# One weight tile and three general tiles more, paid for with a smaller reserve for software DMA descriptors, and other prices in a list scheduler

## The chip, the cores and the metric

One core of one Trainium2 chip runs the whole kernel in one launch. The metric is device microseconds of that core. The engines are called as in the profile: PE (TensorE, matmuls), PEld (its weight loads), DVE (VectorE), ACT (ScalarE), POOL (GpSimd, which here only issues DMAs) and SP (SyncE, which only issues DMAs). A measurement of this kernel tells a difference of about 0.3% from none.

## The reference, cut to what matters

The input is 512 tokens of width 1024, with 16 learned meta tokens ahead of them, so T = 528. Two layers run after one another.

```python
for l in range(DEPTH):                                # DEPTH = 2
    n = rms_norm(h, mix_norm_g[l])
    proj = jnp.einsum("btd,de->bte", n, w_in[l])      # q, k, v, indexer qi/ki/wi, xr, yg, cv, gates gt
    attn = dsa_attention(q, k, v, qi, ki, wi)         # indexer scores, top-128 keys, softmax
    rnn  = rg_lru_branch(xr, yg, ...)                 # conv 4, block-diagonal gates, scan
    cnv  = conformer_conv_branch(cv, ...)             # GLU, depthwise conv 31, LayerNorm, swish
    merged = (g_attn * jnp.einsum("bte,ed->btd", attn, w_o_attn[l])
              + g_rnn * jnp.einsum("bte,ed->btd", rnn, w_o_rnn[l])
              + g_conv * jnp.einsum("bte,ed->btd", cnv, w_o_conv[l]))
    h = h + jnp.einsum("btd,de->bte", merged, w_out[l])
    f = rms_norm(h, ffn_norm_g[l])
    a = jax.nn.silu(f @ w_ffn_gate[l]) * (f @ w_ffn_up[l])
    h = h + a @ w_ffn_down[l]
return h[:, N_META:]
```

All of it is float32, and nearly all of the arithmetic is in products of activations with weights.

## The kernel before, in words

**Layout.** Activations lie transposed: 128 channels on the partitions, 528 tokens (512 in the second layer, after its projections of keys and values) along the free axis. A weight block of 128 output channels by 1024 input channels is one DRAM transfer of 512 KB into a tile of 128 x 1024.

**Products in three passes.** A float32 operand is split into a high part, rounded to float32r, and a low part, the rest. `gemm` (L554 on) multiplies, for each of the 8 slices of 128 input channels, the weight's high part with both parts of the activation (L568: two matmuls, or with 528 columns two of 264 columns for each, so 32 of 264 columns in a weight block), and then, in a second pass over the 8 slices, the weight's low part with the activation's high part (L578: 16 of 264 columns). The products of the conformer's output and of most of the feed-forward layer go through `seven` (L609 high, L613 low), a seven-product scheme on half-size blocks, whose factors are formed from four quarter blocks.

**How a weight comes in.** `weights_in` lets SP load the block into one of two `raw` tiles (L397). `weights_split` takes a `w` tile, and ACT copies the block into it, rounded (the high part, L376). Then it takes a second `w` tile for the low part. For some blocks DVE subtracts (L379). For the others (`by_dma`) ACT writes the negative of the raw block into the tile, and POOL issues a software DMA (L400) that reads the same block from DRAM once more and adds it on the way. There are four `w` tiles, so two weights. `gemm` gives the high part's tile back after the first pass and the low part's after the second:

```python
            hi = yield Alloc("w", 1, FR)
            yield act(hi[:, :k], r[:, :k], AF.Copy, [r], [hi])
            hbox.set(hi)
            lo = yield Alloc("w", 1, FR)
            ...
                yield act(lo[:, :k], r[:, :k], AF.Copy, [r], [lo], scale=-1.0)
                free(r)
                yield add_dma(lo[:, :k], src, [], [lo])
```

In `seven` the low parts of three of the seven factors come by the same kind of DMA, into general `s` tiles (128 x 528, 77 of them), which hold nearly everything else too.

**What sets the order.** Nothing is ordered by hand. Every piece of work is a generator that yields either an operation with a price in ns or a request for tiles. `Sched.run` plays these streams against a clock for each engine: it takes the operation that could start first, or, within 40 ns and on the same engine, the one of the best priority, issues its instruction, and moves that engine's clock by the price. Prices of PE, DVE and ACT come from the tile's width. For a transfer it keeps one clock of bytes moved, at 360 bytes per ns, and holds the result to be there 1900 ns (`MOVE_LAT`) later. A freed tile is handed out oldest first. What comes out is a fixed program for each engine; on the chip only semaphores hold an instruction back. So the prices change no arithmetic, only in which order each engine's instructions stand and which tile each uses.

**The projection of the values.** At the start of each layer `v_gemm` (L856 on) first computes one number per token (L865, `pr`, in half a PSUM bank), which DVE turns into `rtok` (L386); then it accumulates the values (L891) in five half banks. A half bank that `pr` has used is given to it only when `rtok` has been read out.

Of the kernel before, what the change touches and what calls it, by code (L numbers as in the profile page):

```python
# [38 lines left out]
B_OA, B_OR, B_OC, B_OUT, B_FG, B_FU = 71, 79, 87, 95, 103, 125  # L39


NS, NU = 77, 4
NRAW, NW = 2, 4
KEEP = 11
FIRST = 2
EARLY = 4
# [71 lines left out]
TABLES = {"Exp": ("e",), "Tanh": ("e", "g", "s"), "Gelu_apprx_tanh": ("g",), "Silu": ("s",), "Sqrt": ("q",),  # L118
          "Abs_reciprocal_sqrt": ("a",)}
TABLE_LOAD = 1283.0  # L120
MOVE_LAT = 1900.0
SELF = {"PE": 0.0, "DVE": 125.0, "ACT": 110.0, "SP": 0.0, "POOL": 0.0}
LAT = {"PE": 170.0, "DVE": 100.0, "ACT": 130.0, "SP": 0.0, "ACTQ": 0.0, "POOL": 0.0}

# [1 line left out]
class Sched:  # L126
# [80 lines left out]
    def run(self):  # L207
        while self.streams:
            moved = True
            while moved:  # L210
                moved = False
                for s in sorted(self.streams, key=lambda s: s[:2]):
                    r = s[3]
                    if isinstance(r, Box):
                        if r.done:
                            self.step(s, r.v)
                            moved = True
                            break
                    elif isinstance(r, Alloc) and r.kind in ("pp", "b1"):
                        b = self.bank(r.kind, r.keep)  # L220
                        if b is not None:
                            self.step(s, b)
                            moved = True
                            break
                    elif isinstance(r, Alloc):
                        free = self.slots[r.kind]
                        if len(free) >= r.n + (r.keep() if callable(r.keep) else r.keep):
                            got = []
                            for dt in r.dts:
                                at, i = heapq.heappop(free)  # L230
                                b = Buf(r.kind, i, self.make(r.kind, i, dt))
                                b.rd = at + 60.0
                                got.append(b)
                            self.step(s, got if r.many else got[0])
                            moved = True
                            break
            cands = []
            for s in self.streams:
                if isinstance(s[3], Op):
                    ready, t = self.start(s[3])  # L240
                    pen = max(0.0, TABLE_LOAD * (PEN_S if s[3].tab == ("s",) else PEN) - AGE * (t - ready)) if s[3].tab and self.table not in s[3].tab else 0.0
                    cands.append((t + pen, s, t))
            if not cands:
                if not self.streams:
                    return
                raise RuntimeError("nothing can go on: " + ", ".join(
                    f"{s[2].__name__}:{s[3].kind + str(s[3].n) if isinstance(s[3], Alloc) else 'box'}" for s in self.streams))
            first = min(cands, key=lambda c: c[0])
            e, until = first[1][3].eng, first[0] + WINDOW
            t0, s, t = min((c for c in cands if c[1][3].eng == e and c[0] <= until), key=lambda c: c[1][:2])  # L250
            op = s[3]
            cost = op.cost
            if op.tab:
                if self.table not in op.tab:
                    self.table = op.tab[0]
                    cost += TABLE_LOAD
            op.fn()
            end = t + cost
            self.clock[e] = end
            done = end  # L260
            if op.bytes:
                self.moved = max(self.moved, end + 650.0) + op.bytes / 360.0
                done = self.moved + MOVE_LAT
            for b in op.R:
                b.rd = max(b.rd, done + LAT[e])
            for b in op.W:
                b.ready, b.eng = max(b.ready, done), e
            self.step(s, None)
# [10 lines left out]
def trunk(ctx, tc, xT, wt, wv, wd, wg, gain_in, par_in, cst_in, id_in, out):  # L279
    nc = tc.nc  # L280
    V, S, PE = nc.vector, nc.scalar, nc.tensor
# [108 lines left out]
        return Op("DVE", cost, fn, R, W)  # L390

    def pe(cost, fn, R, W):
        return Op("PE", cost, fn, R, W)

    def dma(o, i, R, W, q="SP"):
        e = {"SP": nc.sync, "POOL": nc.gpsimd}[q]
# [157 lines left out]
    def gemm(wbox, nk, xs, cols, epi, prio, need="", keep=0, tail=0, ks=range(NF)):  # L554

        n = cols[1] * cols[2]
        bufs = (yield alloc(need, FT, keep)) if need else []
        hi = yield wbox[0]
        ps = yield psa(cols)
        cuts = [0, nk - tail, nk] if tail < nk else [*range(nk + 1)]  # L560
        for k0, k1 in zip(cuts[:-1], cuts[1:]):
            for k in ks[k0:k1]:
                xh, xl = yield xs[k]

                def go(k=k, xh=xh, xl=xl):
                    for i, b in enumerate((xh, xl)):
                        for o, x in by_part(ps, b, cols):
                            PE.matmul(o, hi[:, 128 * k:128 * k + 128], x, start=(k == ks[0] and i == 0), stop=False)  # L568
                yield pe(2 * n / 2.336, go, [hi, xh, xl], [ps])
            if k1 == nk and k0 < k1:  # L570
                free(hi)
            lo = yield wbox[1]
            for k in ks[k0:k1]:
                xh, _ = xs[k].v

                def go(k=k, xh=xh):
                    for o, x in by_part(ps, xh, cols):
                        PE.matmul(o, lo[:, 128 * k:128 * k + 128], x, start=False, stop=k == ks[nk - 1])  # L578
                yield pe(n / 2.336, go, [lo, xh], [ps])
        free(lo)  # L580
        spawn(epi(ps, psv(ps, cols), *bufs), prio)

    def seven(wb, qs, cols, epi, prio, need):
# [7 lines left out]
        for i in (1, 6, 2, 7, 5, 4, 3):  # L591
            wh, wl = yield wb[i]
            if i in (6, 5):
                pair[i] = pair[{6: 2, 5: 4}[i]] = yield Alloc("b1" if near else "pp")
            ps = pair[i] if i in pair else (yield Alloc("b1"))
            if i in pair:
                h = int(i in (6, 5))
                d = ps[:, h * n:h * n + n] if near else ps[:, h, :n]
            else:
                d = ps[:, :n]  # L600
            q = []
            for c in range(4):
                q.append((yield qs[c])[i])
            R = [t for x in q for t in x[:2]]

            def hi(w=wh, d=d, q=q):
                for c, (h, l, o) in enumerate(q):
                    for e, t in enumerate((h, l)):
                        PE.matmul(d, w[:, 128 * c:128 * c + 128], t[:, o:o + n], start=c == 0 and e == 0, stop=False)  # L609

            def lo(w=wl, d=d, q=q):
                for c, (h, l, o) in enumerate(q):
                    PE.matmul(d, w[:, 128 * c:128 * c + 128], h[:, o:o + n], start=False, stop=c == 3)  # L613
            yield pe(8 * n / 2.336, hi, R + [wh], [ps])
            yield pe(4 * n / 2.336, lo, R + [wl], [ps])
            free(wh, wl)
            done[i].set((ps, d))
# [1133 lines left out]

def build(shapes):
    import concourse.bacc as bacc
    nc = bacc.Bacc("TRN2", target_bir_lowering=False, num_devices=1)
    args = [nc.dram_tensor(f"in_{n}_dram", s, FT, kind="ExternalInput").ap() for n, s in zip(_NAMES, shapes)]
    out = nc.dram_tensor("out_0_dram", (NC, 128, T - NM), FT, kind="ExternalOutput").ap()
    with tile.TileContext(nc) as tc:
        trunk(tc, *args, out)
    return nc
# [8 lines left out]
```

## Time and profile before

| | |
|---|---|
| three runs | 2170.46, 2175.06, 2175.31 us; median 2175.06 |
| the profiled execution | 2181.13 us; its span 2179.3 us |
| granted TensorE clock, mean | 0.991 |
| busy: PE / PEld / DVE / ACT / POOL | 2103.5 / 1974.2 / 1587.6 / 1364.8 / 318.4 us |
| DMA | 342.68 MB, mean 157 GB/s |
| software DMA queue / SP's queue | 145.47 MB / 194.76 MB |
| the chain that ended last | PE 68%, DMA 14% (all of it `w<-in_wt_dram`), issue 10%, DVE 3%, ACT 3% |

The profile is of one execution; a sum made from its rows stands against its 2181.13 us, which is 6.1 us above the median of the runs. A matmul record's duration overlaps that of the next (they are pipelined), so a matmul's price is read from how many start in a full stretch, and not from its own duration. An idle stretch of an engine is given with what ended it.

### The profile page before, as it was taken

The page shows a single profiled execution, that of the slowest core. Times are in us where ns is not written, and L with a number is a line of the kernel's source. Part 1 is how long each engine was busy: PE and PEld are TensorE (multiplying, and loading weights), DVE is VectorE, ACT ScalarE, POOL GpSimd, SP SyncE. Part 2 cuts the span into 40 slices and gives each one's busy share as a digit, 9 for nine tenths or more (in the row PEclk, how much of TensorE's full clock was granted, in tenths as well). Part 3 has the DMA queues.
Part 4 walks back from the last instruction along what each step waited for, and adds up shares of the span by engine and source line. Part 5 has one row for each costly group of instructions (what it writes and reads, how often), then busy time and mean ns, then how long its engine had stood idle before and what let it go on. Part 6 is the DMA issues. An engine that isn't in the chain of part 4 may idle for free.

```text
span 2179.3 us, 38132 instructions
## 1 busy us (share of the span) xinstructions
PE 2103.5 (97%) x14808; PEld 1974.2 (91%) x14808; DVE 1587.6 (73%) x2990; ACT 1364.8 (63%) x2113; POOL 318.4 (15%) x392
## 2 busy tenths in 40 slices
PE   6989999999999999999999899999999999999999
PEld 6889999999999999999989888988877887899997
DVE  7699987997237487677668999889972465767674
ACT  6556878876565465555457478888765645655452
POOL 1112110111111011111111111111111110111120
PEclk9999999999999999999999999999999999999999
DMA  8468654788887486576466686568888966766563
GB/s 229 101 142 187 144 120 104 172 175 170 174 202 184 120 184 148 131 169 165 103 186 144 148 186 138 122 133 170 181 178 182 214 156 140 181 151 158 148 143 107
DMA packets 127045, 342.68 MB, mean 157 GB/s; under 512 B 14864, under 2 KB 17040, under 8 KB 126864
## 3 DMA queue, kind: packets, MB, share of 16 engines
q0 software_dynamic: 50112, 145.47, 37.6%
q1 hardware_dynamic: 76608, 194.76, 30.7%
q8 instruction: 116, 1.90, 0.3%
q14 instruction: 65, 0.53, 0.1%
q10 hardware_dynamic: 144, 0.02, 0.0%
HBM read 327.91 MB, written 4.26 MB: 152 GB/s over the span
## 4 chain that ended last, share of the span: by engine, by line
PE 68%; DMA 14%; issue 10%; DVE 3%; ACT 3%; POOL 1%; POOLq 0%; DVEq 0%; ACTq 0%
PE banks L568 28%; PE banks L578 16%; DMA w<-in_wt_dram 14%; PE banks L609 11%; PE banks L613 6%; PE banks L1346 1%; PE banks L891 1%; DVE s L379 1%; PE banks L953 1%; PE banks L1325 1%; ACT w L376 1%; ACT s L376 1%; PE banks L962 1%; PE banks L1086 1%; DVE mx L1003 1%
## 5 line engine op out<-in xcount | busy, mean ns | idle before, releaser
L568 PE MATMUL banks<-s,w 128*128 128x264 f32 (+1 forms) x6432 | 1032.6, 313 | 12.8 <-ACT w L376 7.1
L568 PEld LDWEIGHTS banks<-s,w 128*128 128x128 f32 x6432 | 907.5, 190 | 80.8 <-ACT w L376 7.1
L376 ACT ACTIVATE w<-raw 128x1024 fp32r<-128x1024 f32 (+3 forms) x486 | 480.5, 993 | 338.9 <-PE banks L568 131.9
L578 PE MATMUL banks<-s,w 128*128 128x264 f32 (+1 forms) x3216 | 554.3, 317 | 34.0 <-DMA w<-in_wt_dram 33.5
L578 PEld LDWEIGHTS banks<-s,w 128*128 128x128 f32 x3216 | 463.5, 191 | 79.7 <-DMA w<-in_wt_dram 46.5
L376 ACT ACTIVATE s<-s 128x512 fp32r<-128x512 f32 (+8 forms) x640 | 379.7, 614 | 90.4 <-DVE s L379 68.3
L379 DVE TENSOR_TENSOR s<-s,s 128x528 f32<-128x528 f32 (+9 forms) x522 | 329.5, 656 | 59.2 <-ACT s L376 39.5
L379 DVE TENSOR_TENSOR s<-s,banks 128x512 f32<-128x512 f32 (+3 forms) x340 | 195.4, 588 | 225.2 <-PE banks L578 128.4
L400 POOL DMA_DIRECT2D w<-in_wt_dram x192 | 167.2, 871 | 1262.4 <-ACT w L376 1110.7
L382 DVE SCALAR_TENSOR_TENSOR s<-s,half,s 128x512 f32<-128x512 f32 (+22 forms) x480 | 344.0, 745 | 3.6 <-ACT s L376 0.3
L609 PE MATMUL banks<-s,s 128*128 128x264 f32 (+1 forms) x2464 | 346.0, 283 | 0.4 <-DVE s L379 0.3
L609 PEld LDWEIGHTS banks<-s,s 128*128 128x128 f32 x2464 | 317.9, 188 | 2.4 <-DVE s L379 0.8
L376 ACT ACTIVATE s<-banks 128x528 f32<-128x528 f32 (+11 forms) x338 | 165.0, 505 | 127.5 <-PE banks L578 49.0
L376 ACT ACTIVATE s<-u 128x512 fp32r<-128x512 f32 x176 | 110.5, 628 | 182.3 <-DVE u L379 167.1
L613 PE MATMUL banks<-s,s 128*128 128x264 f32 (+1 forms) x1232 | 199.0, 284 | 6.9 <-DMA s<-in_wt_dram 6.9
L400 POOL DMA_DIRECT2D s<-in_wt_dram x132 | 113.8, 862 | 514.1 <-ACT s L376 343.8
L613 PEld LDWEIGHTS banks<-s,s 128*128 128x128 f32 x1232 | 168.9, 188 | 8.7 <-DMA s<-in_wt_dram 7.5
L379 DVE TENSOR_TENSOR s<-u,s 128x512 fp32r<-128x512 f32 x176 | 119.8, 688 | 33.6 <-ACT s L376 31.0
L382 DVE SCALAR_TENSOR_TENSOR s<-s,banks 128x528 f32<-128x528 f32 (+1 forms) x48 | 33.4, 696 | 117.4 <-PE banks L578 117.3
L376 ACT ACT_TABLE_LOAD x80 | 102.6, 1283 | 4.9 <-DMA s<-in_xT_dram 3.6
L379 DVE TENSOR_TENSOR w<-raw,w 128x512 fp32r<-128x512 f32 (+2 forms) x94 | 75.5, 811 | 5.3 <-ACT w L376 4.4
L379 DVE TENSOR_TENSOR u<-s,s 128x512 f32<-128x512 f32 x88 | 60.3, 686 | 24.5 <-DMA s<-in_wt_dram 24.5
(128 smaller groups left out, 1278.9 us busy)
## 6 DMA issues: line engine op xcount, KB each, us to landing
raw<-in_wt_dram SPq DMA_DIRECT2D x206, 512.0 KB, 4.3
w<-in_wt_dram POOLq DMA_DIRECT2D x192, 512.0 KB, 7.7
s<-in_wt_dram SPq DMA_DIRECT2D x176, 256.0 KB, 5.0
s<-in_wt_dram POOLq DMA_DIRECT2D x132, 256.0 KB, 4.5
raw<-in_wd_dram SPq DMA_DIRECT2D x64, 256.0 KB, 3.7
raw<-in_wd_dram SPq DMA_DIRECT2D x16, 384.0 KB, 3.8
s<-s POOLq DMA_DIRECT2D x36, 132.0 KB, 7.3
s<-in_xT_dram SPq DMA_DIRECT2D x16, 264.0 KB, 4.8
```

The costliest lines, as they stand in the source:

```text
L376: return Op("ACT", cost, lambda: S.activation(o, i, f, **kw), R, W, TABLES.get(name))
L379: return Op("DVE", 69 + width(o) / 0.96, lambda: V.tensor_tensor(o, a, b, op), R, W)
L382: return Op("DVE", (69 if isinstance(s, float) else 129) + width(o) / 0.96, lambda: V.scalar_tensor_tensor(o, a, s, b, op0, op1), R, W)
L400: return Op("POOL", 1040.0, lambda: nc.gpsimd.dma_start(out=o, in_=i, accum_op=ALU.add), R, W, None, 4 * o.shape[0] * width(o))
L568: PE.matmul(o, hi[:, 128 * k:128 * k + 128], x, start=(k == ks[0] and i == 0), stop=False)
L578: PE.matmul(o, lo[:, 128 * k:128 * k + 128], x, start=False, stop=k == ks[nk - 1])
L609: PE.matmul(d, w[:, 128 * c:128 * c + 128], t[:, o:o + n], start=c == 0 and e == 0, stop=False)
L613: PE.matmul(d, w[:, 128 * c:128 * c + 128], h[:, o:o + n], start=False, stop=c == 3)
L891: PE.matmul(ps[:tn, :264], a[:, t0:t0 + tn], b[:, o:o + 264], start=e + part + k == 0 and a is nh, stop=bool(e and part and k == 3))
L953: PE.matmul(ps[:, :w], a, b[:, :w], start=e == 0, stop=e == n - 1)
L962: PE.matmul(ps[:, c, :hw], a, b[:, c * hw:(c + 1) * hw], start=e == 0, stop=e == n - 1)
L1003: yield dve(70 + w / 0.96, lambda: V.max(mx[rows], sv[rows]), [sc], [])
```

## The change

Three things are edited, and the builder's one argument that makes room.

- `dynamic_dma_scratch_size=4096`: the part of every SBUF partition that is set aside for the descriptors of POOL's software DMAs. Without the argument it is 16384 bytes. So 12288 bytes become free in each partition.
- `NW` goes from 4 to 5 and `NS` from 77 to 80: one `w` tile (1056 x 4 = 4224 bytes a partition) and three `s` tiles (3 x 528 x 4 = 6336 bytes), 10560 bytes together.
- The scheduler's prices: all of PE's times 1.066; a transfer moves 310 bytes per ns on SP's queue and 210 on POOL's, and is there 2000 ns after that on SP's and 4300 ns on POOL's.

```diff
-NS, NU = 77, 4
-NRAW, NW = 2, 4
+NS, NU = 80, 4
+NRAW, NW = 2, 5
...
-MOVE_LAT = 1900.0
+MOVE = {"SP": (310.0, 2000.0), "ACTQ": (310.0, 2000.0), "POOL": (210.0, 4300.0)}
...
             if op.bytes:
-                self.moved = max(self.moved, end + 650.0) + op.bytes / 360.0
-                done = self.moved + MOVE_LAT
+                rate, lat = MOVE[op.eng]
+                self.moved = max(self.moved, end + 650.0) + op.bytes / rate
+                done = self.moved + lat
...
     def pe(cost, fn, R, W):
-        return Op("PE", cost, fn, R, W)
+        return Op("PE", 1.066 * cost, fn, R, W)
...
-    nc = bacc.Bacc("TRN2", target_bir_lowering=False, num_devices=1)
+    nc = bacc.Bacc("TRN2", target_bir_lowering=False, num_devices=1, dynamic_dma_scratch_size=4096)
```

The number of instructions of each kind stays: the same matmuls, the same 328 additions by DMA on POOL, the same 532 transfers on SP; ACT has one table load more. From L262 on, line numbers are one higher in the changed kernel (`act` L377, `tt` L380, the matmuls L569, L579, L610 and L614). The order of nearly every stretch differs somewhere. Two places follow.

The first is ACT, in the first layer's merge of a branch's output, with 528 columns. `wN_M` is `w` tile N, with M the number of the allocation; `raw` is the loaded block; each block is copied twice, first the high part, then the low part; `s<-banks` is the emptying of a bank. Before:

```order
L376 ACTIVATE w2_6644<-raw1_6558 128x1024
L376 ACTIVATE s25_6605<-banks_83 128x528
L376 ACTIVATE w3_6662<-raw1_6558 128x1024
L376 ACTIVATE w0_6700<-raw0_6612 128x1024
L376 ACTIVATE w1_6718<-raw0_6612 128x1024
L376 ACTIVATE w2_6758<-raw1_6673 128x1024
L376 ACTIVATE s68_6719<-banks_83 128x528
L376 ACTIVATE w3_6776<-raw1_6673 128x1024
```

And now:

```order
L377 ACTIVATE w4_6609<-raw1_6539 128x1024
L377 ACTIVATE w0_6646<-raw1_6539 128x1024
L377 ACTIVATE s25_6610<-banks_83 128x528
L377 ACTIVATE w1_6667<-raw0_6592 128x1024
L377 ACTIVATE w2_6702<-raw0_6592 128x1024
L377 ACTIVATE w3_6723<-raw1_6650 128x1024
L377 ACTIVATE w4_6760<-raw1_6650 128x1024
L377 ACTIVATE s11_6724<-banks_83 128x528
```

Before, high parts use tiles 0 and 2 and low parts tiles 1 and 3, so a low part follows the low part of two weights earlier in its tile; now the five tiles go round, a low part follows a high part, and the emptying of a bank stands behind the low part's copy instead of ahead of it.

The second place is DVE in the first layer, ahead of `rtok`. The first row scales the last of the eight channel blocks of the input for the norm; the rows with `s19` or `s20` (cosines and sines) and the rows after them rotate the indexer's queries and split them in two. Before:

```order
L382 SCALAR_TENSOR_TENSOR s8_610<-s15_119,neg_80,s49_324 128x528
L379 TENSOR_TENSOR s51_405<-s51_405,s19_130 128x528
L379 TENSOR_TENSOR s52_406<-s52_406,s20_134 128x528
L379 TENSOR_TENSOR s50_612<-s8_610,s2_611 128x528
L379 TENSOR_TENSOR s51_405<-s51_405,s52_406 128x528
L379 TENSOR_TENSOR s61_485<-s61_485,s19_130 128x528
L379 TENSOR_TENSOR s62_486<-s62_486,s20_134 128x528
L379 TENSOR_TENSOR s53_407<-s51_405,s53_407 64x528
L379 TENSOR_TENSOR s54_408<-s51_405,s54_408 64x528
L379 TENSOR_TENSOR s61_485<-s61_485,s62_486 128x528
L386 TENSOR_SCALAR rtok_574<-banks_83 128x4
```

And now:

```order
L383 SCALAR_TENSOR_TENSOR s42_603<-s15_119,neg_80,s45_300 128x528
L380 TENSOR_TENSOR s47_318<-s47_318,s48_319 128x528
L387 TENSOR_SCALAR rtok_595<-banks_83 128x4
L340 SCALAR_TENSOR_TENSOR sp_p_267<-sp_p_267,sp_y_266 128x16
L380 TENSOR_TENSOR s44_605<-s42_603,s43_604 128x528
```

Between the last channel's scaling (from `s15_119`, the eighth input tile) and `rtok` stood nine rows, and now stands one.

## Rows read from the trace of the kernel before

**Rows 1.** The page, busy time of the engines.
```profile
PE 2103.5 (97%) x14808; PEld 1974.2 (91%) x14808; DVE 1587.6 (73%) x2990; ACT 1364.8 (63%) x2113; POOL 318.4 (15%) x392
```

**Rows 2.** Waits of PE: us in total, times, longest us.
```profile
PE banks L578 <- DMA w<-in_wt_dram: 33.5, 30, 3.9
PE banks L891 <- DVE rtok L386: 13.7, 1, 13.7
PE banks L568 <- ACT w L376: 7.1, 1, 7.1
PE banks L613 <- DMA s<-in_wt_dram: 6.9, 7, 1.7
PE banks L568 <- ACT s L376: 4.1, 4, 1.6
PE banks L962 <- DVE s L382: 3.5, 1, 3.5
```

**Rows 3.** Timeline around one wait: start us, us, engine line op [idle before <-releaser].
```profile
541.06 4.07 PE L568 MATMUL banks<-s,w 128*128 128x264 f32 x32
541.26 0.62 ACT L376 ACTIVATE s<-banks 128x528 f32<-128x528 f32 x1 [0.30 <-PE banks L578]
541.76 1.05 ACT L376 ACTIVATE w<-raw 128x1024 fp32r<-128x1024 f32 x1
...
543.11 0.86 POOL L400 DMA_DIRECT2D w<-in_wt_dram  x1 [6.36 <-ACT w L376]
...
552.25 2.21 PE L578 MATMUL banks<-s,w 128*128 128x264 f32 x16 [0.41 <-DMA w<-in_wt_dram]
```

**Rows 4.** Instructions on tile `w`: duration ns min/median/max; then issue to landing.
```profile
L376 ACT ACTIVATE w<-raw x486: 612/1057/1089, 6.0 to 2165.6; 128x1024 fp32r<-128x1024 f32 x134, 128x512 fp32r<-128x512 f32 x22, 128x768 fp32r<-128x768 f32 x4, 128x1056 fp32r<-128x1056 f32 x2
...
DMA to landing us min/median/max: 5.6/7.7/9.4
```

**Rows 5.** Windows: PE, PEld, DVE, ACT, POOL busy (x), PEclk, DMA share, GB/s.
```profile
871.70:926.20 54.50, 54.50 (x450) 54.50 (x449) 37.99 (x65) 28.33 (x52) 9.05 (x11) 1.00 0.58 131
1688.90:1743.40 54.50, 52.89 (x289) 45.06 (x288) 26.89 (x49) 33.21 (x55) 10.34 (x12) 1.00 0.91 214
```

**Rows 6.** Waits of ACT.
```profile
ACT w L376 <- PE banks L578: 68.3, 71, 4.9
```

**Rows 7.** The page, DMA queues (packets, MB, share) and issues (KB, us to landing).
```profile
q0 software_dynamic: 50112, 145.47, 37.6%
q1 hardware_dynamic: 76608, 194.76, 30.7%
...
raw<-in_wt_dram SPq DMA_DIRECT2D x206, 512.0 KB, 4.3
w<-in_wt_dram POOLq DMA_DIRECT2D x192, 512.0 KB, 7.7
```

**Rows 8.** Windows at half clock, just behind five of the waits for `w`.
```profile
29.20:32.60 3.40, 3.40 (x18) 3.40 (x17) 2.31 (x4) 0.14 (x1) 0.00 (x0) 0.51 0.88 194
121.40:124.80 3.40, 3.40 (x13) 2.99 (x13) 3.17 (x14) 1.75 (x3) 0.00 (x0) 0.50 0.82 192
1230.70:1240.90 10.20, 8.96 (x41) 8.97 (x42) 8.16 (x20) 2.85 (x4) 0.88 (x1) 0.50 0.74 182
1790.50:1793.90 3.40, 3.40 (x9) 2.64 (x8) 1.01 (x2) 0.29 (x1) 0.00 (x0) 0.50 0.00 0
1852.00:1855.40 3.40, 3.40 (x9) 2.63 (x8) 0.14 (x1) 0.14 (x1) 0.00 (x0) 0.50 1.03 275
```

**Rows 9.** Timeline of the first layer's value projection.
```profile
53.01 0.76 DVE L382 SCALAR_TENSOR_TENSOR s<-s,neg,s 128x528 f32<-128x528 f32 x1
53.69 6.00 DVE L379 TENSOR_TENSOR s<-s,s 128x528 f32<-128x528 f32 x9
59.61 0.15 DVE L386 TENSOR_SCALAR rtok<-banks 128x4 f32<-128x4 f32 x1
...
59.82 2.57 PE L891 MATMUL banks<-w,s 128*128 128x264 f32 x10 [13.73 <-DVE rtok L386]
```

## The prediction

> **What bounds the kernel now.** I read the page's busy times first: PE is busy for 2103.5 of 2179.3 us and no other engine for more than 1587.6, PEld apart, which works for PE [rows 1]. So PE is the bound, the change leaves its matmuls as they are, and a gain can only come from time in which PE stands still or runs slowly. The view of PE's waits comes next [rows 2]. Two rows make most of it: 33.5 us in 30 waits of the low-part pass for the low part's own DMA, and one wait of 13.7 us in the first layer's value projection for `rtok`. A smaller one of 6.9 us in 7 waits is the same DMA in the seven-product scheme. The other long ones add up to 7.1 + 4.1 + 3.5 = 14.7 us, of which 7.1 is the start.
>
> Why the low part is late shows in one wait taken apart [rows 3]. The pass that frees the tile ends when the next high pass starts, at 541.06. ACT first empties a bank, and copies the raw block at 541.76; POOL's DMA starts at 543.11; PE goes on at 552.25, after 0.41 us of standing. So 2.0 us pass from the free tile to the DMA, and 9.1 us until it has landed. For all such tiles the copy takes 1.06 us and the landing 7.7 us in the median, 9.4 at most [rows 4].
>
> Against that stands the time which PE's work leaves. A full stretch holds 450 matmuls in 54.5 us, all of 264 columns there [rows 5], so one costs 121.1 ns, 0.459 ns a column. With four tiles a low part takes the tile of the low part two weights earlier; from that tile's last use to the next use of it PE does a high pass, a low pass and a high pass: 32 + 16 + 32 = 80 matmuls, 9.69 us. The chain without the emptying of a bank is 1.06 + 7.7 and, from [rows 3], about 0.3 between copy and DMA and 0.2 ahead of the copy: 9.3 us. There is 0.4 us to spare in the median, and 1.3 us too little when the landing takes 9.4. That is the size of the waits (33.5 / 30 = 1.1 us). And it is the tile that the copy waits for, not the raw block: ACT waits 71 times, 68.3 us, for the low pass that frees it [rows 6].
>
> **The change part by part.** The fifth `w` tile: in the order now, the low part follows a high part in its tile. Between lie a low, a high, a low and a high pass, 96 matmuls or 11.63 us, 1.94 us more. Counted over the whole order at 0.459 ns a column, 123 of the 196 low parts by DMA had under 10.5 us before, and 7 have now. With 9.3 needed in the median and 11.0 with the longest landing, the spare time is 2.3 us and 0.6. The waits' mean of 1.1 us lies below the 1.94 gained; only waits over that, the longest 3.9, should leave a rest. Of 33.5 us I leave 4 for those and the seven short ones: **29.5 us** gained. The bounds are 0 (the landing grows by as much as the window) and 33.5.
>
> The three `s` tiles and POOL's latency of 4300 ns in the prices: both start the low parts of `seven` earlier. Its waits are at most 1.7 us long [rows 2], so I take **5 us** of the 6.9; the bounds are 0 and 6.9.
>
> The clock: behind five of the waits for `w` lie stretches with a granted clock of 0.50 or 0.51, that is 1.2 GHz in place of 2.4, in which PE was busy for 3.40 + 3.40 + 8.96 + 3.40 + 3.40 = 22.6 us [rows 8]. At full clock that work takes half, so 11.3 us were lost. They follow the longest of the waits, which go or shrink; I take **8 us**, between 0 and 11.3.
>
> `rtok`: DVE had nine operations, 6.00 us, between the last channel's scaling and `rtok` [rows 9], and now has one; eight of 0.67 us are 5.3 us. Some small operations of 16 columns have moved ahead instead, so I take **4.5 us** off the wait of 13.7, between 0 and 13.7. The rest stays: the values' second half bank is still one that `pr` had.
>
> The prices alone, without the tiles, remove no work. They bring another order everywhere, and the trace of before cannot show what waits that order has. I take the waits that the change isn't aimed at, 14.7 us [rows 2], as the measure: at worst they double, at best they go. I charge **7 us** for new ones, between -14.7 and +14.7. One table load more on ACT is an operation on an engine that is busy for 63% of the span; PE doesn't see it, and if it did it would cost under 2 us.
>
> The smaller reserve: 0. No view shows it. What the rows show is that the software queue's 50112 packets [rows 7] belong to 388 DMAs (328 additions and 60 copies), 129 each, and that in [rows 3] a new one comes about every 5.8 us (a weight's 48 matmuls) with a landing of 7.7: one or two stand open at a time. Below, a rival says what it costs if the reserve holds less than that. By the Trainium skill (DMA: Bandwidth & Descriptors, "The descriptor swizzle") a 128-partition transfer takes 9 read and 9 write descriptors on each engine, and a descriptor has 16 bytes; an estimate from that page is 256 descriptors in the new reserve, some 28 transfers, and the cost nothing too. No run here shows a descriptor.
>
> **The sum.** 29.5 + 5 + 8 + 4.5 - 7 = 40 us. The profiled execution's 2181.1 us would become 2141; against the median of the runs, 2175.06, it is **2135 us**.
>
> **The rivals.** *The landing grows with the window.* More DMAs stand open at once, and in 1688 to 1743 us the 16 DMA engines are already busy for 0.91 of the time [rows 5]; the same 512 KB take 4.3 us on SP's queue and 7.7 on POOL's [rows 7]. If each landing takes 1.9 us longer, the waits for `w` and the half clock stay and only 5 + 4.5 us are gained: 2165 us. Against it: no byte is added, and over the span the two queues keep the DMA engines busy for 37.6% + 30.7% = 68% [rows 7].
>
> *The tile isn't what is short.* If the DMA landed quickly, the low part would come late because its raw block did, and there are still two of those. Then the fifth tile does nothing, and `rtok` alone is left: 2170.5 us. Against it are the 7.7 us and the copy's 71 waits for PE [rows 4, 6]. The Trainium skill speaks for it (DMA: Bandwidth & Descriptors, "Anatomy of one DMA"): its fit of 2.0 us and a time by bytes is, for 512 KB, an estimate of 3.2 us. By that the chain would be 4.8 us, four tiles would do, and the sum would be this rival's. The trace has more than twice as much for a DMA that adds, and it decides.
>
> *The order gives it back.* DVE and ACT are queues in order, and one badly placed operation can hold PE as `rtok` did, 13.7 us and then a slow clock. Three such places take the whole gain, about 2175 us; with four the kernel is slower. For it: every stretch is put in another order. Against it: before, with prices further from the trace's, one such place was found.
>
> *The reserve holds POOL back (slower).* If POOL may not start a DMA until the one before has landed, a weight can't come in under 7.7 us, where PE needs one each 5.8. For 196 low parts that is 196 x 1.9 = 370 us: 2545 us. It decides from the point where the reserve holds less than two transfers. For it speaks only that a quarter of the reserve is left; against it, 129 packets a transfer.
>
> **How the numbers follow.** The forecast has 0.74, with a range of its own from 2112 (33.5 + 6.9 + 11.3 + 4.5, and 7 of the other waits) to 2155 (half of the gain). The landing rival has 0.10, the tile rival 0.04, the order 0.08 (0.05 within 0.3%, 0.03 slower), the reserve 0.04. The range reaches to the landing rival's 2165 and one microsecond on, and to 2110: 0.10 and nearly all of 0.74 lie in it. About 0.3%, 6.5 us, is what a measurement of this kernel tells from no change. Faster: 0.74 + 0.10 = 0.84. Within: 0.04 + 0.05 = 0.09. Slower: 0.03 + 0.04 = 0.07.
>
> **What would show it.** Right: PE's waits for DMA `w` under 10 us together, for `s` under 3, `rtok` near 9; the landing still near 7.7 us; fewer half-clock stretches; PE busy for about the same time within 15 us in a shorter span. Wrong: a landing near 9.6 us with the waits as they were (the first rival), ACT's weight copies held by raw blocks (the second), a new row of more than 10 us among PE's waits (the third), POOL waiting for DMAs of its own (the fourth).

## The result and the profile after

The changed kernel takes 2147.39 us in the median of 4 runs (2145.93 to 2148.31), the kernel before 2174.22 in the median of 4. The ratio is 0.9879 with a 95% interval of 0.9862 to 0.9896: 26.8 us faster. Forecast were 2135 us (40 us faster) and a range of 2110 to 2166. Run once more beside other kernels, the changed one took 2147.70 us with a ratio of 0.9863 (0.9845 to 0.9881).

The profiled execution took 2148.31 us. Its page begins so:

```profile
span 2146.5 us, 37980 instructions
...
PE 2093.8 (98%) x14808; PEld 1972.3 (92%) x14808; DVE 1591.3 (74%) x2990; ACT 1361.0 (63%) x2114; POOL 318.8 (15%) x392
```

The span is 32.8 us shorter than the one before, and PE's busy time is 9.7 us shorter [rows 1], with the same 14808 matmuls; so PE's idle time fell by 23.1 us. The busy time that went lies in the low passes, whose row on the page of before and on the page of after is:

```profile
L578 PE MATMUL banks<-s,w 128*128 128x264 f32 (+1 forms) x3216 | 554.3, 317 | 34.0 <-DMA w<-in_wt_dram 33.5
L579 PE MATMUL banks<-s,w 128*128 128x264 f32 (+1 forms) x3216 | 543.6, 313 | 11.5 <-DMA w<-in_wt_dram 11.5
```

The view of PE's waits (us in total, times, longest us):

```profile
PE banks L579 <- DMA w<-in_wt_dram: 11.5, 5, 3.3
PE banks L569 <- ACT w L377: 7.3, 1, 7.3
PE banks L569 <- ACT s L377: 5.6, 4, 2.2
PE banks L892 <- DVE rtok L387: 5.0, 1, 5.0
PE banks L569 <- DVE s L383: 4.8, 3, 3.1
PE banks L614 <- DMA s<-in_wt_dram: 2.8, 2, 1.6
PE banks L610 <- DVE s L380: 2.5, 1, 2.5
PE banks L610 <- ACT s L377: 2.5, 3, 1.9
```

Against [rows 2], the waits for a low part's DMA went from 33.5 us in 30 to 11.5 in 5, those of the seven-product scheme from 6.9 to 2.8, and `rtok` from 13.7 to 5.0. Other rows are new or longer: waits for ACT and DVE, each of a few microseconds. Summed over all rows of the view, waits were 71.1 us before and are 48.7 now.

The additions by DMA land no sooner than in [rows 4]; this is the last line of the answer on tile `w`:

```profile
DMA to landing us min/median/max: 6.0/7.8/9.9
```

So the waits went because the tile is free earlier, not because the transfer is faster. ACT now stands where it didn't before: 32.9 us in 18 waits of weight copies for a block of `in_wt` in a `raw` tile. The clock, in contrast, gained little. These are all the stretches of the changed kernel's run at half clock (us, PE busy (x), PEld, DVE, ACT, POOL busy (x), PEclk, DMA share, GB/s), but for one behind the last matmul:

```profile
28.80:32.20 3.40, 3.40 (x18) 3.40 (x16) 3.36 (x10) 1.98 (x4) 0.00 (x0) 0.51 0.89 192
49.20:56.00 6.80, 5.79 (x26) 5.79 (x27) 6.18 (x16) 2.57 (x4) 0.00 (x0) 0.50 0.48 111
110.70:114.10 3.40, 3.40 (x15) 3.40 (x16) 3.29 (x11) 1.29 (x3) 0.00 (x0) 0.50 0.64 166
138.00:141.40 3.40, 3.40 (x18) 3.40 (x17) 3.40 (x10) 0.15 (x1) 0.45 (x1) 0.50 1.02 240
312.10:315.50 3.40, 3.40 (x14) 3.01 (x13) 1.14 (x3) 1.71 (x5) 0.00 (x0) 0.50 0.45 90
1192.70:1196.10 3.40, 3.40 (x14) 3.11 (x13) 3.40 (x12) 1.06 (x1) 0.27 (x1) 0.50 1.05 274
1742.20:1745.60 3.40, 3.40 (x18) 3.40 (x17) 1.30 (x3) 0.00 (x0) 0.00 (x0) 0.51 0.98 222
```

PE was busy for 26.2 us in them. Before it was 29.4: the 22.6 of [rows 8], and two more stretches, behind `rtok` and behind a wait of 3.46 us for DVE:

```profile
49.70:63.40 13.70, 3.58 (x16) 3.58 (x17) 12.10 (x23) 5.13 (x8) 0.00 (x0) 0.50 0.22 53
131.60:135.00 3.40, 3.27 (x15) 3.27 (x16) 3.40 (x8) 3.26 (x4) 0.00 (x0) 0.51 0.66 119
```

Three of the seven now (28.8, 138.0 and 1192.7) still stand behind waits for `w`, of 1.87, 2.44 and 2.66 us, and one behind `rtok`. The other three stand behind other waits: 110.7 behind one of 3.06 us for DVE, 312.1 behind one of 1.84 us for ACT (before, a wait of 1.64 us for ACT had no slow stretch behind it), 1742.2 behind two of 1.60 and 1.90 in the seven-product scheme. A wait need not be followed by a slow stretch: behind the longest now, 3.30 us, there is none. And one execution is a thin basis: in the changed kernel's second profile, below, three of these stretches are missing, though the waits ahead of them are nearly the same, and one has come behind a wait of 4.71 us; in all PE was busy for some 22 us in them.

Most of what is left of the waits for `w` has another cause than the tile. This is the timeline ahead of the longest, rows of ACT, POOL and PE:

```profile
1194.84 1.06 ACT L377 ACTIVATE w<-raw 128x1024 fp32r<-128x1024 f32 x1 [3.04 <-DMA raw<-in_wt_dram]
...
1201.77 0.82 ACT L377 ACTIVATE s<-s,par,half 128x512 f32<-128x512 f32 x1 [5.87 <-DVE s L383]
1202.60 1.28 ACT L377 ACT_TABLE_LOAD   x1
...
1205.18 1.04 ACT L377 ACTIVATE w<-raw 128x1024 fp32r<-128x1024 f32 x1
...
1206.52 0.86 POOL L401 DMA_DIRECT2D w<-in_wt_dram  x1 [13.54 <-ACT w L377]
...
1214.92 1.24 PE L579 MATMUL banks<-s,w 128*128 128x264 f32 x8 [3.30 <-DMA w<-in_wt_dram]
```

ACT stands for 5.87 us at the convolution's first operation, which waits for DVE. The copies of the weight stand behind it in ACT's queue, and the DMA starts only at 1206.52, though the window of 11.6 us that the tile leaves began near 1200. It lands 8.4 us later, when PE has waited 3.30.

The kernel before had this too, at the same place, and its longest wait for `w` stood behind it:

```profile
1218.02 0.82 ACT L376 ACTIVATE s<-s,par,half 128x512 f32<-128x512 f32 x1 [6.31 <-DVE s L382]
...
1231.94 3.89 PE L578 MATMUL banks<-s,w 128*128 128x264 f32 x16 [3.85 <-DMA w<-in_wt_dram]
```

Two more waits for `w` follow stands of ACT for DVE in the same way, in either kernel. With this one they were 2.66 + 1.92 + 3.85 = 8.4 us before (at 120.87, 1200.80 and 1231.94) and are 2.44 + 2.66 + 3.30 = 8.4 now (at 137.17, 1191.64 and 1214.92). That is read from the timelines; an experiment below takes one of these stands away. So of the 33.5 us nearly all of the other 25.1 went: 3.1 are left.

### The profile page after: what moved, and what is told of

It reads as the page before. It is cut to its first block, busy times and chain, and to the rows that moved or that the text cites. A ratio compares the mean times of both kernels' runs of the same rounds, so it can differ in the third digit from the quotient of the medians.

```text
span 2146.5 us, 37980 instructions
## 1 busy us (share of the span) xinstructions
PE 2093.8 (98%) x14808; PEld 1972.3 (92%) x14808; DVE 1591.3 (74%) x2990; ACT 1361.0 (63%) x2114; POOL 318.8 (15%) x392
## 4 chain that ended last, share of the span: by engine, by line
PE 69%; DVE 10%; ACT 3%; issue 2%; DMA 1%; POOL 0%; SPq 0%; DVEq 0%; ACTq 0%; POOLq 0%
PE banks L569 31%; PE banks L579 15%; PE banks L610 12%; PE banks L614 6%; DVE s L383 3%; DVE s L380 3%; ACT s L377 2%; DVE mx L1004 1%; PE banks L1347 1%; DMA s<-in_wt_dram 1%; DVE s L1005 1%; PE banks L954 1%; PE banks L1087 1%; PE banks L1326 1%; DVE u L1005 1%
## 5 line engine op out<-in xcount | busy, mean ns | idle before, releaser
L569 PE MATMUL banks<-s,w 128*128 128x264 f32 (+1 forms) x6432 | 1033.4, 313 | 17.7 <-ACT w L377 7.3
L569 PEld LDWEIGHTS banks<-s,w 128*128 128x128 f32 x6432 | 906.5, 189 | 85.3 <-ACT w L377 7.3
L377 ACT ACTIVATE w<-raw 128x1024 fp32r<-128x1024 f32 (+3 forms) x486 | 479.0, 990 | 286.0 <-PE banks L569 137.5
L579 PE MATMUL banks<-s,w 128*128 128x264 f32 (+1 forms) x3216 | 543.6, 313 | 11.5 <-DMA w<-in_wt_dram 11.5
L579 PEld LDWEIGHTS banks<-s,w 128*128 128x128 f32 x3216 | 461.5, 190 | 47.7 <-DMA w<-in_wt_dram 13.1
L377 ACT ACTIVATE s<-s 128x512 fp32r<-128x512 f32 (+8 forms) x640 | 382.7, 615 | 175.4 <-DVE s L380 137.0
L380 DVE TENSOR_TENSOR s<-s,s 128x528 f32<-128x528 f32 (+8 forms) x522 | 331.0, 654 | 48.6 <-ACT s L377 41.0
L610 PE MATMUL banks<-s,s 128*128 128x264 f32 (+1 forms) x2464 | 347.3, 283 | 5.0 <-DVE s L380 2.5
L383 DVE SCALAR_TENSOR_TENSOR s<-s,half,s 128x512 f32<-128x512 f32 (+23 forms) x480 | 339.8, 743 | 2.8
L610 PEld LDWEIGHTS banks<-s,s 128*128 128x128 f32 x2464 | 318.5, 189 | 7.9 <-ACT s L377 3.1
L380 DVE TENSOR_TENSOR s<-s,banks 128x512 f32<-128x512 f32 (+3 forms) x340 | 195.5, 587 | 110.8 <-PE banks L614 67.6
L377 ACT ACTIVATE s<-banks 128x528 f32<-128x528 f32 (+11 forms) x338 | 165.0, 505 | 155.2 <-PE banks L614 75.4
L614 PE MATMUL banks<-s,s 128*128 128x264 f32 (+1 forms) x1232 | 198.5, 283 | 2.8 <-DMA s<-in_wt_dram 2.8
L377 ACT ACTIVATE s<-u 128x512 fp32r<-128x512 f32 x176 | 110.4, 627 | 102.3 <-DVE u L380 87.4
L614 PEld LDWEIGHTS banks<-s,s 128*128 128x128 f32 x1232 | 169.5, 189 | 3.2 <-DMA s<-in_wt_dram 3.2
L380 DVE TENSOR_TENSOR s<-u,s 128x512 fp32r<-128x512 f32 x176 | 119.7, 688 | 47.1 <-ACT s L377 42.9
L380 DVE TENSOR_TENSOR w<-raw,w 128x512 fp32r<-128x512 f32 (+2 forms) x94 | 76.1, 814 | 62.7 <-PE banks L569 40.8
L380 DVE TENSOR_TENSOR u<-s,s 128x512 f32<-128x512 f32 x88 | 60.3, 685 | 25.7 <-DMA s<-in_wt_dram 25.7
```

Source lines behind the costliest of these rows:

```text
L377: return Op("ACT", cost, lambda: S.activation(o, i, f, **kw), R, W, TABLES.get(name))
L380: return Op("DVE", 69 + width(o) / 0.96, lambda: V.tensor_tensor(o, a, b, op), R, W)
L383: return Op("DVE", (69 if isinstance(s, float) else 129) + width(o) / 0.96, lambda: V.scalar_tensor_tensor(o, a, s, b, op0, op1), R, W)
```

## The experiments

Two theories stood against each other: the fifth `w` tile makes the gain (**tile theory**), or the order that the new prices make (**price theory**); a smaller rival was the three `s` tiles. Ratios are to the kernel before, run beside each; the brackets are 95% intervals.

**The fifth `w` tile alone**, with the small reserve, on the kernel before:

```diff
-NRAW, NW = 2, 4
+NRAW, NW = 2, 5
...
-    nc = bacc.Bacc("TRN2", target_bir_lowering=False, num_devices=1)
+    nc = bacc.Bacc("TRN2", target_bir_lowering=False, num_devices=1, dynamic_dma_scratch_size=4096)
```

> Only the fifth w tile (and the smaller reserve that makes room for it); 77 s tiles and the old prices stay. Tile theory: a low part's tile is free 1.94 us of PE work earlier, so PE's waits for the low part's DMA fall from 33.5 us to 5 to 12 us, the half-clock stretches behind them shrink, rtok's wait stays at 13.7 us or so, and the time is 2145 to 2155 us. Price theory (the order made by the new prices brings the gain): 2165 to 2176 us, with 25 us or more of waits for w left.

Measured: 2154.73 us, ratio 0.9904 (0.9881 to 0.9927). Waits for `w` 9.0 us in 6, `rtok` 11.8. The tile theory holds: this edit alone gives some 21 us. One of its signs is missing: the half-clock stretches did not shrink, PE was busy for some 37 us in them in the profiled execution, which took 2161.51 us, the longest of the six. Runs spread from 2151.55 to 2161.51 us, more than those of the changed kernel.

**The new prices alone**: 77 `s` tiles, 4 `w` tiles and the default reserve, with the three price edits of the change.

> Only the new prices; 77 s tiles, 4 w tiles and the old reserve stay. Tile theory: 121 of the 196 low parts still have a window under 10.5 us (123 before), so PE's waits for w stay at 25 to 35 us; rtok's wait falls towards 5 to 9 us, which the order does; the time is 2158 to 2172 us. Price theory: 2145 to 2155 us, with waits for w under 15 us.

Measured: 2188.96 us, ratio 1.0061 (1.0039 to 1.0082). Both theories had it faster than before, and it is slower. `rtok` fell to 2.8 us as the order promised, but the waits for `w` grew:

```profile
PE banks L579 <- DMA w<-in_wt_dram: 39.0, 32, 6.3
PE banks L569 <- ACT w L377: 7.3, 1, 7.3
PE banks L610 <- DVE s L380: 6.1, 4, 2.3
```

The longest, 6.3 us, lies at the same place as the one taken apart above; the second, of 6.07, lies at the same operation in the first layer. ACT's view of the stretch from 1200 to 1215 us has one row, the convolution's operation again:

```profile
ACT s L377 <- DVE s L383: 8.2, 1, 8.2
```

Here ACT stands for 8.2 us, and with four tiles the chain of [rows 3, 4] has only 0.4 us to spare. That fits the longer waits for `w`, but doesn't account for the 12.6 us by which this kernel is slower: all waits together are 72.5 us, against 71.1 in the kernel before, because `rtok` gave back about what `w` and others took. Where the time went is open.

**Both kinds of tiles, old prices** (`NS, NU = 80, 4`, `NRAW, NW = 2, 5` and the reserve of 4096):

> The fifth w tile and the three s tiles with the old prices. Tile theory: within 4 us of the kernel with the fifth w tile alone, and the 6.9 us of waits for s fall under 3 us. Rival (the general tiles matter): 8 us or more below the kernel with the w tile alone. If the prices are worth nothing, this kernel is as fast as the changed one, 2147 us; if they cost something, it is below it.

Measured: 2152.36 us, ratio 0.9894 (0.9870 to 0.9918). Waits for `w` 9.2 us, for `s` 5.4, not under 3. It is within 2.4 us of the `w` tile alone. The changed kernel's two ratios, 0.9879 and 0.9863, lie below by 3 and 7 us, but the intervals overlap: on top of the tiles, what the prices are worth can't be told from nothing.

**The three `s` tiles alone** (`NS, NU = 80, 4` and the reserve):

> Only the three s tiles (and the smaller reserve); 4 w tiles and the old prices stay. Tile theory: waits for w as before, 28 to 36 us, and the time 2166 to 2176 us. Rival (the general tiles matter): 2160 us or less.

Measured: 2176.36 us, ratio 0.9994 (0.9978 to 1.0009). Waits for `w` 33.9 us, for `s` 3.3. Nothing, as the tile theory has it.

The next four ran together. The first is the changed kernel again:

> The changed kernel once more, beside the three kernels that follow. 2145 to 2151 us, a ratio to the kernel before of 0.986 to 0.990. If the new prices are worth something on top of the tiles, the ratio stays below the 0.9894 of the tiles with the old prices by 0.002 or more; if it comes within 0.0015 of it, they are worth nothing that can be told.

Measured: 2147.70 us, ratio 0.9863, as told above; it lies 0.0031 below the tiles with the old prices, but that one ran at another time, with an interval of 0.0024 to each side. Its profile shows how much one execution differs from the next with the same program: waits for `w` are 14.4 us in 8, the longest 4.7, where the first had 11.5 in 5; all waits are 48.2 us against 48.7.

**The convolution's first operation on DVE**, to take away what ACT stood at:

```diff
-                yield act(y[:, m0:T], u[:, m0:T], AF.Identity, [u], [y], scale=hc_(l, P_DWW + 240, c), bias=pc(l, P_DWB, c))
+                yield ts(y[:, m0:T], u[:, m0:T], hc_(l, P_DWW + 240, c), pc(l, P_DWB, c), ALU.mult, ALU.add, [u], [y])
```

> The changed kernel with the convolution's first operation (scale and bias of the newest tap) on DVE in place of ACT. In the changed kernel it is the operation at which ACT stands for 5.9 us near 1196 to 1202 us, with a weight's low part queued behind it. Theory (what is left of the waits for w comes from ACT held up by one operation in its queue, not from tiles): the waits for w fall from 11.5 us to 8 or less, the one of 3.3 us near 1211 us goes, and the time is 3 to 8 us shorter than the changed kernel's. Rival (what is left is the DMA's landing): the waits stay at 9 to 13 us and the time within 3 us.

Measured: 2145.23 us, ratio 0.9851 (0.9832 to 0.9871), 2.5 us below the changed kernel beside it and not to be told from it. The wait near 1211 us is gone, but the waits for `w` are 16.7 us in 13 now, against 14.4 in 8 in the changed kernel beside it: the list scheduler made another order and smaller waits came up elsewhere. That ACT's stand made that one wait is borne out; that it is a lever for the time is not.

**`rtok` in a stream of its own:**

```diff
-            yield ts(rt_, pr[:, :4], -0.5 * IDX_SCALE, None, ALU.mult, None, [pr], [])
-            free(pr)
-            rtok.set(rt_)
+            def tok():
+                yield ts(rt_, pr[:, :4], -0.5 * IDX_SCALE, None, ALU.mult, None, [pr], [])
+                free(pr)
+                rtok.set(rt_)
+            spawn(tok(), 1)
```

> The changed kernel with rtok's one DVE operation in a stream of its own of high priority, so that it stands earlier in DVE's order. Theory (the wait for rtok and the slow clock behind it are DVE's order alone): the wait of 5.0 us goes or falls under 1.5 us, the half-clock stretch of 6.8 us near 49 us goes, and the time is 5 to 8 us shorter. Rival (something else is late right behind rtok, the second half of the normed input): another wait takes its place, and less than 2 us are gained.

Measured: 2147.51 us, ratio 0.9856 (0.9837 to 0.9874), the same as the changed kernel. `rtok` is down to 1.2 us, and others are longer:

```profile
PE banks L569 <- DVE s L383: 8.2, 2, 4.3
...
PE banks L1213 <- DVE s L383: 2.1, 1, 2.1
PE banks L957 <- ACT vmeta L377: 2.1, 1, 2.1
...
PE banks L895 <- DVE rtok L387: 1.2, 1, 1.2
```

The rival holds, though not with the wait that it named: the row of waits for DVE went from 4.8 us in the changed kernel to 8.2. All waits together did fall, from 48.2 us to 44.4, and the slow stretch near 49 us is gone; but PE was busy for some 28 us at half clock, against 22 in the changed kernel beside it, and its busy time grew by 4.3 us.

**A sixth `w` tile** (`NRAW, NW = 2, 6` and `dynamic_dma_scratch_size=1024` in the changed kernel):

> The changed kernel with a sixth w tile, paid for with a reserve of 1024 bytes. Theory (the tile is not short any more): within 4 us of the changed kernel, with 8 to 14 us of waits for w. Rival (the window is still what is short): waits for w under 5 us and 6 us or more gained. If the reserve of 1024 bytes held POOL back, POOL's issue of an addition would take longer than 0.87 us, or start later.

Measured: 2136.28 us, ratio 0.9813 (0.9794 to 0.9831), the fastest of all: 11.4 us below the changed kernel beside it, with intervals apart. Neither theory said this: waits for `w` stay, as the first had it, and the time falls, as the second had it. The smaller reserve shows nowhere: POOL's issue of an addition takes 0.88 us in the mean against 0.87, and its waits for an addition are all for other engines or for DMAs.

```profile
PE banks L579 <- DMA w<-in_wt_dram: 9.3, 6, 2.8
PE banks L569 <- ACT w L377: 7.2, 1, 7.2
PE banks L892 <- DVE rtok L387: 4.0, 1, 4.0
PE banks L963 <- ACT s L377: 3.6, 3, 1.5
```

All waits together are 41.8 us, against 48.2 in the changed kernel beside it. At half clock there are only two stretches ahead of the end:

```profile
47.60:54.40 6.80, 3.84 (x17) 3.85 (x18) 6.69 (x13) 4.34 (x7) 2.02 (x3) 0.50 0.83 178
184.20:187.60 3.40, 3.40 (x15) 3.40 (x16) 3.40 (x7) 3.40 (x6) 0.78 (x1) 0.50 0.88 149
```

PE is busy for 7.2 us in them, where the changed kernel had 26.2 in its first profile and some 22 in the one beside this; the mean granted clock is 0.997 against 0.994. Against the one beside it the profiled span is 10.5 us shorter, 6.5 of it PE's idle time and 4.0 its busy time. Half of 22 - 7.2, some 7 us, should have come from the clock; that is an estimate, and PE's busy time shows no more than the 4.0.

The last four ran together too. **The reserve alone** (4096 bytes in the kernel before, nothing else):

> The kernel before with the reserve of 4096 bytes and nothing else: the same order on every engine, the same number of tiles, only their addresses differ. Theory (the reserve costs nothing): a ratio of 0.997 to 1.003, the landing of the additions 7.7 us in the median, no new wait of POOL. Rival (it holds POOL back): slower by 0.5% or more.

Measured: 2177.74 us, ratio 1.0006 (0.9994 to 1.0018), landing 5.5/7.7/9.4 us. It costs nothing that can be told.

**A reserve of 320 bytes** in the changed kernel (`dynamic_dma_scratch_size=320`):

> The changed kernel with a reserve of 320 bytes in place of 4096, the tiles and the order as in the changed kernel. If the reserve bounds how many software DMAs stand open, this one is slower, and POOL's issues of additions start later or take longer than 0.87 us; with one open at a time it would be near 2520 us, as the prediction's rival has it (370 us on top), with two open at a time within 40 us of the changed kernel. If the reserve bounds nothing, it is within 6 us of the changed kernel.

Measured: 2315.70 us, ratio 1.0664 (1.0625 to 1.0703), 168 us over the changed kernel; between the cases that were named. POOL's view of waits has rows that say "issue", time in which it waited for nothing that the profile shows:

```profile
POOL w L401 <- ACT w L377: 422.8, 57, 55.6
POOL w L401 <- ACT s L377: 414.0, 70, 13.5
POOL w L401 <- issue: 287.4, 56, 8.6
POOL s L401 <- ACT s L377: 234.9, 59, 5.7
POOL s L401 <- issue: 90.2, 19, 7.1
```

PE's waits for `w` are 89.6 us in 44. So at 320 bytes the reserve does bound what POOL may have open. Counted from the issues and landings in the trace, 358 of POOL's 388 transfers start when none of its others is open and 30 beside one, never more; in the changed kernel 299 start beside one or more, up to five, and with 1024 bytes 299 do too, up to five. This is the prediction's rival with one transfer open at a time, but at 168 us, not 370: that sum took each landing at 7.7 us, and here it is 5.9. With 5.9 the same sum makes some 20 us, so it also left something out; it counts none of POOL's 192 other transfers.

**Six `w` tiles, old prices** (80 `s` tiles, a reserve of 1024 bytes):

> Six w tiles and 80 s tiles with a reserve of 1024 bytes, and the old prices. If the gain of the sixth tile is the tile's (more room between a late operation on ACT and PE, and so fewer waits that are followed by a slow clock), this one is within 5 us of the kernel with six tiles and the new prices, 2136 us, or a ratio of 0.979 to 0.984. If it needs the new prices' order, the ratio is that of the five tiles with the old prices, 0.987 to 0.991.

Measured: 2144.90 us, ratio 0.9867 (0.9848 to 0.9887). Waits for `w` are 6.1 us in 3, fewer than with the new prices, but `rtok` stands at 13.6, where the old prices had 13.7 with four tiles and 11.8 with five:

```profile
PE banks L891 <- DVE rtok L386: 13.6, 1, 13.6
```

It is 0.5% slower than the same tiles with the new prices, with intervals apart: the sixth tile's gain needs their order. `rtok` is the row that tells the two apart: 9.6 us of it, where all waits differ by 8.0 (49.8 against 41.8) and PE's busy time by 0.7. Over five tiles with the old prices (0.9894) the sixth gains nothing that can be told.

**Seven `w` tiles, 77 `s` tiles**, new prices, a reserve of 1024 bytes:

> Seven w tiles and 77 s tiles with a reserve of 1024 bytes and the new prices. If room ahead of PE is still what is short, waits for w fall under 7 us and the ratio is below 0.979. If six tiles are enough, the ratio is 0.979 to 0.985, and with three s tiles fewer the waits for s go back to 5 to 8 us.

Measured: 2164.15 us, ratio 0.9948 (0.9933 to 0.9962), slower than five or six. Waits for `w` fall as expected, and the others take their place:

```profile
PE banks L610 <- DVE s L380: 8.4, 5, 2.6
PE banks L569 <- ACT w L377: 7.1, 1, 7.1
PE banks L614 <- DMA s<-in_wt_dram: 5.6, 6, 1.9
PE banks L579 <- DMA w<-in_wt_dram: 4.2, 3, 1.9
```

All waits are 53.8 us, 12.0 more than with six tiles. The larger part is in PE's busy time, 15.4 us longer: nine stretches stand at half clock ahead of the end, with some 34 us of PE's work, where six tiles had 7.2. Whether it is the three `s` tiles that are missing or the order was not told apart.

## Why the prediction was right, and where it was off

The forecast case came true, with two thirds of its gain. By its steps, profile against profile:

| step of the prediction | forecast, us | measured, us |
|---|---|---|
| fifth `w` tile: waits for `w` | 29.5 | 33.5 - 11.5 = 22.0 |
| `s` tiles and POOL's price: waits for `s` | 5 | 6.9 - 2.8 = 4.1 |
| clock behind the waits for `w` | 8 | (22.6 - 10.2) / 2 = 6.2 |
| clock behind all other waits | not counted | (6.85 - 15.99) / 2 = -4.6 |
| `rtok` | 4.5 | 13.7 - 5.0 = 8.7 |
| new waits of the new order | -7 | -12.4 |
| reserve | 0 | 0 (ratio 1.0006) |

The new waits are all rows other than those three: 71.1 - 33.5 - 6.9 - 13.7 = 17.0 us before, 48.7 - 11.5 - 2.8 - 5.0 = 29.4 now. The measured column adds up to 24.0 us, while the two profiled spans differ by 32.8. Of the 8.8 us between them 8.1 are PE's shorter busy time (9.7, less the clock's 6.2 - 4.6 = 1.6) and 0.7 idle time in gaps too short for the view. The two rows of the low passes shown above say where the busy time went: 10.7 us, while no other row of PE moved by more than 2.2. The row is 550.4 us or more in all four profiles with four `w` tiles and 547.1 or less in all with five or more (the reserve of 320 bytes apart). Part of it is the clock. The rest fits short waits that the profile counts as PE's busy time, since PEld's waits for `w`, 46.5 us on the page before and 13.1 on the page after, fell by 11.4 us more than PE's own; no row shows such a wait by itself. If so, the tile gave more than the 22.0 in the table, and that it comes nearer to the forecast 29.5 is luck: the prediction had only the waits of the view in its sum. The profiled execution of before was itself some 7 us above the median, which is why 32.8 became 26.8.

- **The tile was the right step, and the experiments bear it out.** Alone it gives 21 us; the `s` tiles and the reserve alone give none. The window argument held in its core: the landing stayed at 7.8 us and the waits went. The rest was undersized, 11.5 us where 4 were left, and the sign "under 10 us" did not come. The step that had it wrong is the one that took all 30 waits for the tile's, by their mean of 1.1 us: 8.4 us of them followed stands of ACT, could be seen in the trace of before, and are there unchanged. The tile's own rest is 3.1 us. The chain of 9.3 us was summed from [rows 3, 4] with 0.2 us ahead of the copy, as if ACT were free for it; where ACT stands for 5.87 us, 1.94 us of room can't take that up.
- **The clock** was right in size for the stretches behind the waits for `w`, 6.2 us of 8. What failed is that the charge for new waits had no clock in it: the stretches behind all other waits grew, and 1.6 us are left. "Fewer half-clock stretches" did not come either, there were seven and are seven. And the term was read from one execution: the kernel with the reserve alone, which has the order of the kernel before, had three stretches behind waits for `w` in its profile, not five, and some 20 us of PE's work in all, not 29.4.
- **`rtok`** gained twice the forecast, and half of that is luck. The eight operations fewer were right: `rtok` now comes 1.3 us after the last channel's scaling began, where [rows 9] have 6.6. But that scaling itself starts at 48.70 instead of 53.01, which the sum hadn't counted.
- **The prices** were taken as neutral with a charge of 7 us; the new waits were 12.4. At four `w` tiles the prices cost 0.6%, at five they can't be told from nothing, at six they gain 0.5%. Why their order is bad with four tiles is open, but for the longer waits for `w` behind ACT's stands; with six the gain stands in `rtok`'s row, 9.6 us.
- **The rivals.** The growing landing is out (7.7 to 7.8 us). In the changed kernel an addition into `w` takes 7.7 to 7.8 us in the median whether none, one, two or more of POOL's other transfers are open meanwhile. That the tile wasn't short is out as the bound, since the tile alone gave 21 us; but that rival's sign, copies held by raw blocks, has come up behind it, 32.9 us of ACT's time. With this rival goes the sum by the Trainium skill's fit (DMA: Bandwidth & Descriptors, "Anatomy of one DMA"): the trace of the change has 7.8 us again where an estimate from the page gave 3.2. The order that gives back is partly true, 12.4 us; and the prediction's count of one badly placed operation before was short, as ACT's stand of 6.31 us was another. The reserve that holds POOL back exists as a mechanism, but at 320 bytes, not at 4096. That "one or two" additions stand open was a little low: before, up to five others were open when a transfer of POOL's started.

## What to carry to other kernels

Where an engine that bounds the kernel waits for a buffer's refill, write down two times: what the refill takes from the moment the buffer is free, and how much of the bounding engine's work lies in between. Here 9.3 stood against 9.7 us, and one buffer more was worth 1%. Before counting the gain as the whole of the waits, look for each of the long ones at which in-order queue the refill passes through; what is late there stays late. Here that was 8.4 of 33.5 us, and the trace of before had the rows. And where a scheduler makes the order, a single edit measures the edit and a new order together: try it with and without its companions, as the prices show, that are worse than nothing alone.

## What the runs showed of the hardware that was not expected

- A wait of PE can cost more than its length, by the clock, but need not. Behind the wait of 3.06 us at 110.66 PE worked for 3.40 us at half clock, an estimated 1.7 us lost. With the same program the wait near 28 us was followed by such a stretch in one execution (1.87 us) and not in the other (1.60), and so was the one near 1191.6 (2.66 and 2.45).
- With the reserve of 320 bytes an addition into `w` lands 5.9 us after its issue in the median, against 7.8. None of those 192 had another of POOL's transfers beside it; but neither had 17 in the changed kernel, and they took 7.7. So the company of POOL's own transfers is not the reason, and what is stays open.
- Three quarters of the reserve for software DMA descriptors could be given up at no cost (ratio 1.0006 at 4096 bytes), and at 1024 bytes the fastest kernel of all ran.
